# A kernel's own scheduler: small tiles tracked by the column, and fp32r matmuls counted as n + 32 cycles

## The chip, the cores and the metric

The kernel runs on one core of one Trainium2 chip. The metric is the device time of one execution in microseconds; the time before is 2639.61 us, the median of three runs (2639.43 to 2639.66).

## The reference, cut to what matters

Two transformer blocks follow each other on x of 256 tokens by 2048 channels, all in float32. The first has an input projection to 11,264 columns, a gated linear recurrence (HGRN2) and a banded attention with 8 heads each, two projections, an output projection and a feed-forward part of width 5632. The second takes a condition c, multiplies silu(c) by a 2048 x 12288 matrix, and uses the six pieces as shift, scale and gate:

```python
mod = jax.nn.silu(c) @ w_ada[l] + b_ada[l]
shift_m, scale_m, gate_m, shift_f, scale_f, gate_f = jnp.split(mod, 6, axis=-1)
h = modulate(rms_norm_2(x, pre_norm_mix[l]), shift_m, scale_m)
...                      # h @ w_in, two attention mixers with 8 heads each -> o_n, o_m
o = jnp.concatenate([o_n, o_m], axis=-1) @ w_o[l]
x = x + gate_m[:, None, :] * rms_norm_2(o, post_norm_mix[l])
h = modulate(rms_norm_2(x, pre_norm_ffn[l]), shift_f, scale_f)
f = jnp.square(jax.nn.relu(h @ w_up[l])) @ w_down[l]
x = x + gate_f[:, None, :] * rms_norm_2(f, post_norm_ffn[l])
```

Here w_o is 2048 x 2048, w_up 2048 x 8192 and w_down 8192 x 2048. A norm divides each token's row by the root of its mean square, so it needs the whole row of a product before the next product can begin.

## The kernel before, in words

**Products.** The 256 tokens are two blocks of 128 (tb 0 and 1). Every large product runs in groups of 512 output columns; a group's items are its 128-row chunks of the weight matrix. Activations and weights are each held as two fp32r halves, so an item is three matmuls per token block (`emit`: high by high, high by low, low by high) into an accumulator `acc` in PSUM. Weights come as pairs of chunks, 512 KB by one DMA into one of six `raw` buffers; ScalarE rounds them (`wh`) and VectorE subtracts (`wl`) into a ring of five to seven slots (`split_ahead`). How far ahead a pair is split is set by the count of items (`LA_AT`: 0, 2 or 4 items), not by a clock. Block 1 trails block 0 by `lag` items (14 at the end of w_o, 8 at the start of w_up, 4 elsewhere), at most lag + 6. A group that needs activations of a norm (`need`) waits for them. SP issues all DMAs.

**The planner.** The order on each engine is the order in which this Python program issues instructions, and semaphores keep it right whatever the order. The program issues with a model of the chip: a clock for each engine (`clk`: pe, at, dv, sp, dma), and for each piece of a tile when it was last written and read and by which engine (`wr`, `rd`). `op` starts an instruction when its engine is free and its operands are ready; a result of another engine counts 0.06 us later (`LAT`) beside a tail of 0.1 us (ScalarE, TensorE) or 0.05 us (VectorE). The pieces are 128 columns (`spans`). The costs are formulas: a 512-column VectorE operation is 512/960 + 0.068 = 0.601 us and 0.062 more with a per-row factor; a 512-column ScalarE operation from SBUF 512/1200 + 0.094, and 0.093 more for an accumulated sum; a DMA 1.1 us, then its bytes at 360 GB/s, then 1.5 us.

**Tasks.** Work beside the products is written as generators: each `yield` ends a step. A step is issued when TensorE's planned clock has reached its due time (`due`): after a plain yield, the planned end of what the step before it issued, plus 0.2 us; after `yield "dv"`, VectorE's planned clock less 0.2. `main` tries the splits first, then the tasks (`pump`), then the next item. Negative priorities go first.

**The norms between products.** After w_o (`post7`, `ev7`, `sums7`, lines from the function that opens phase 7): for each block, each 512 columns are squared on ScalarE with the sum into a column of `stat`, and multiplied by the gate on VectorE (og<-acc). Then `row_rstd` works out the factor in `stat`; four updates xr<-og,stat,xr on VectorE alternate with four squares og<-xr on ScalarE, whose sums go to other columns of `stat`; a second `row_rstd` follows; then `norm_mod` spawns four parts, each a scaling (og<-xr,stat, line 241), four transposes on TensorE (line 281), scale and shift, and the split into `hh` and `hl` that w_up's matmuls read. For block 0 the chain is issued in one go, for block 1 with a yield between its steps. `stat` is one tile of 128 x 64.

**gemv.** The product with w_ada runs on VectorE in 192 items of 512 KB (`gemv`, `gload`, tile graw): an item is started no sooner than 4.5 us of TensorE's planned clock after the one before it on a fixed schedule, and is issued when that clock has reached the planned landing of its load. It begins when the recurrence is done.

**Lines that the prediction touches.** Line 276 is the matmul in `mm`, 281 the transpose in `tr`, 220 every activation, 232, 236 and 241 VectorE's two-operand, scalar-and-tensor and scalar operations, 1438 the sum of four in `sum4`, 298 every DMA.

Of the kernel before, what the change touches and what calls it, by code (L numbers as in the profile page):

```python
# [85 lines left out]
class Group:  # L86
    def __init__(self, w, quads, c0, n, lhs, evac, need=None, lag=2, pre=None, name=""):
        self.w, self.quads, self.c0, self.n = w, list(quads), c0, n
        self.lhs, self.evac, self.need, self.lag, self.pre = lhs, evac, need, lag, pre
        self.chunks = [4 * q + j for q in self.quads for j in range(4)]  # L90
        self.acc = {}
        self.name = name
# [7 lines left out]
class Prog:  # L100
# [8 lines left out]
    def __init__(self, tc, ins, out, dbg=None, stop=99):  # L109
        self.tc, self.nc, self.ins, self.out, self.dbg, self.stop = tc, tc.nc, ins, out, dbg or {}, stop  # L110
        self.clk = {"pe": 0.0, "at": 0.0, "dv": 0.0, "sp": 0.0, "dma": 0.0}
        self.now = 0.0
        self.wr, self.rd, self.turn, self.place, self.bank = {}, {}, {}, {}, {}
        self.cur = 0.0
        self.set = None
        self.tasks = []
        self.queue = []
        self.done = set()
        self.hooks = []
        self.limits = {}  # L120
        self.items = []
        self.pairs = []
        self.p = [0, 0]
# [15 lines left out]
    def spans(self, ap):  # L139
        name = ap.tensor.name  # L140
        lo = hi = ap.offset
        for st, n in list(ap.ap)[1:]:
            if st < 0:
                lo += st * (n - 1)
            else:
                hi += st * (n - 1)
        p = self.place.get(name, name)
        return [(p, i) for i in range(lo // 128, hi // 128 + 1)]

    def ready_at(self, aps, eng):  # L150
        t = 0.0
# [117 lines left out]
    def mm(self, out, lhsT, rhs, start=True, stop=True):  # L269
        n = self.width(out)  # L270
        if lhsT.dtype == F32R:
            c = max(n + 6, 257 if n > 128 else 511)
        else:
            c = max(4 * n + 12, 1022 if n < 96 and self.width(lhsT) > 64 else 500)
        self.op("pe", c / 2400.0, [out], [lhsT, rhs])
        self.nc.tensor.matmul(out, lhsT, rhs, start=start, stop=stop)  # L276
# [306 lines left out]
    def tile(self, pool, shape, tag, bufs=1, dtype=F32):  # L583
        self.uid += 1
        t = pool.tile(list(shape), dtype, tag=tag, name=f"{tag}_{self.uid}", bufs=bufs)
        self.slot(t, pool, tag, bufs)
        return t

    def pool(self, name, side):
# [1337 lines left out]
```

## Time and profile before

| | |
|---|---|
| median of three runs | 2639.61 us |
| the profiled execution | 2640.57 us |
| its span, first to last instruction | 2638.8 us |
| mean granted TensorE clock | 0.997 |
| matmul and transpose records on TensorE | 12084 |

The profile is of one execution. A busy TensorE is not one at its peak, since the ends of its matmuls are modelled; the distance between starts tells more. A wait is put down to the engine that came last.

### The profile page before, as it was taken

Reading aid. Unit: us, or ns where it says so; the run is one execution under the profiler, and the core shown is the slowest. Engines: PE = TensorE matmul, PEld = TensorE weight load, DVE = VectorE, ACT = ScalarE, POOL = GpSimd, SP = SyncE. Lnnn points to the kernel's source line nnn. Section 1 sums busy time; section 2 is a strip of 40 time slices with the busy share of each in tenths; the row PEclk is TensorE's granted clock in tenths of the full one; section 3 lists DMA queues with packets and bytes.
Section 4 is the critical chain, followed back from the end, with each engine's and each line's share of the span. In section 5 each row is a group of like instructions: output and inputs, shape, how many; then the busy total and the mean of one; then the engine's idle time right before and its main releaser. Section 6 shows DMA issues by size and latency. Waiting matters only on the chain.

```text
span 2638.8 us, 32635 instructions
## 1 busy us (share of the span) xinstructions
PE 2608.0 (99%) x12084; PEld 2155.7 (82%) x12084; DVE 1733.8 (66%) x2408; ACT 1241.3 (47%) x1756; POOL 0.2 (0%) x4
## 2 busy tenths in 40 slices
PE   8999999999999999999999999999999999999998
PEld 7888888888888888888888887888778888888887
DVE  6665668888778888888854655655554444444445
ACT  7565555444453434333443543554554454453443
POOL 0000000000000000000000000000000000000000
PEclk9999999999999999999999999999999999999999
DMA  7545448888779889998955465345355555556553
GB/s 275 184 143 164 163 155 288 308 296 292 262 243 318 311 296 326 333 333 307 317 194 190 138 225 169 127 136 191 135 185 185 197 182 193 189 180 197 184 183 130
DMA packets 163888, 582.00 MB, mean 221 GB/s; under 512 B 18448, under 2 KB 19984, under 8 KB 163472
## 3 DMA queue, kind: packets, MB, share of 16 engines
q1 hardware_dynamic: 163728, 579.91, 64.4%
q8 instruction: 95, 1.56, 0.2%
q14 instruction: 65, 0.53, 0.1%
HBM read 577.74 MB, written 2.10 MB: 220 GB/s over the span
## 4 chain that ended last, share of the span: by engine, by line
PE 89%; DVE 4%; DMA 4%; ACT 2%; issue 1%; SPq 0%; DVEq 0%; ACTq 0%
PE acc L276 83%; PE s L276 4%; DMA graw<-in_w_ada 3%; PE s L281 2%; DVE wl L232 1%; DVE gacc L236 1%; ACT wh L220 0%; PE d L276 0%; PE d L281 0%; DMA ident<-in_cst 0%; DVE A L267 0%; DMA raw<-in_masks 0%; DMA raw<-in_w_in 0%; ACT evt L220 0%; DVE evt L232 0%
## 5 line engine op out<-in xcount | busy, mean ns | idle before, releaser
L232 DVE TENSOR_TENSOR wl<-raw,wh 128x1024 fp32r<-128x1024 f32 (+2 forms) x875 | 1043.4, 1210 | 543.8 <-ACT wh L220 541.7
L220 ACT ACTIVATE wh<-raw 128x1024 fp32r<-128x1024 f32 (+2 forms) x875 | 897.1, 1047 | 610.4 <-PE acc L276 565.8
L276 PE MATMUL acc<-wh,hh 128*128 128x512 f32 (+2 forms) x1600 | 629.6, 393 | 4.0 <-ACT hh L220 3.4
L276 PE MATMUL acc<-wh,hl 128*128 128x512 f32 (+2 forms) x1600 | 618.2, 386 | 0.9 <-DVE hl L232 0.9
L276 PE MATMUL acc<-wl,hh 128*128 128x512 f32 (+2 forms) x1600 | 617.3, 386 | 1.5 <-DVE wl L232 1.5
L276 PEld LDWEIGHTS acc<-wh,hh 128*128 128x128 f32 x1600 | 301.0, 188 | 67.2 <-issue 5.2
L276 PEld LDWEIGHTS acc<-wh,hl 128*128 128x128 f32 x1600 | 300.7, 188 | 63.4 <-DVE hl L232 2.1
L276 PEld LDWEIGHTS acc<-wl,hh 128*128 128x128 f32 x1600 | 301.3, 188 | 59.0 <-DVE wl L232 2.2
L236 DVE SCALAR_TENSOR_TENSOR gacc<-graw,csilu,gacc 128x512 f32<-128x512 f32 x360 | 269.9, 750 | 45.8 <-DMA graw<-in_w_ada 38.2
L276 PE MATMUL acc<-wh,xh 128*128 128x512 f32 x704 | 282.4, 401 | 6.5 <-ACT wh L220 6.5
L276 PE MATMUL acc<-wl,xh 128*128 128x512 f32 x704 | 275.6, 392 | 0.9 <-DVE wl L232 0.9
L276 PE MATMUL acc<-wh,xl 128*128 128x512 f32 x704 | 275.8, 392 | 0.0
L276 PE MATMUL acc<-wh,uh 128*128 128x512 f32 x512 | 200.0, 391 | 0.0
L276 PE MATMUL acc<-wh,ul 128*128 128x512 f32 x512 | 199.3, 389 | 0.0
L276 PE MATMUL acc<-wl,uh 128*128 128x512 f32 x512 | 199.2, 389 | 0.0
L276 PEld LDWEIGHTS acc<-wh,xh 128*128 128x128 f32 x704 | 133.0, 189 | 32.1 <-ACT wh L220 6.5
L276 PEld LDWEIGHTS acc<-wl,xh 128*128 128x128 f32 x704 | 133.0, 189 | 27.9 <-DVE wl L232 2.1
L276 PEld LDWEIGHTS acc<-wh,xl 128*128 128x128 f32 x704 | 132.7, 188 | 28.2
L276 PE MATMUL acc<-wh,fh 128*128 128x512 f32 x320 | 125.0, 391 | 0.0
L276 PE MATMUL acc<-wh,fl 128*128 128x512 f32 x320 | 124.6, 389 | 0.0
L276 PE MATMUL acc<-wl,fh 128*128 128x512 f32 x320 | 124.5, 389 | 0.0
L276 PEld LDWEIGHTS acc<-wh,ul 128*128 128x128 f32 x512 | 96.1, 188 | 20.0
(283 smaller groups left out, 2426.7 us busy)
## 6 DMA issues: line engine op xcount, KB each, us to landing
raw<-in_w_in SPq DMA_DIRECT2D x255, 512.0 KB, 4.0
graw<-in_w_ada SPq DMA_DIRECT2D x192, 512.0 KB, 5.1
raw<-in_w_ffn_in SPq DMA_DIRECT2D x176, 512.0 KB, 5.0
raw<-in_w_up SPq DMA_DIRECT2D x128, 512.0 KB, 4.2
raw<-in_w_down SPq DMA_DIRECT2D x128, 512.0 KB, 4.2
raw<-in_w_ffn_out SPq DMA_DIRECT2D x88, 512.0 KB, 4.9
raw<-in_w_out SPq DMA_DIRECT2D x32, 512.0 KB, 4.4
raw<-in_w_o SPq DMA_DIRECT2D x32, 512.0 KB, 4.3
```

Of the source, the lines that this page charges most:

```text
L220: self.nc.scalar.activation(out=out, in_=in_, func=func, **kw)
L232: self.nc.vector.tensor_tensor(out=out, in0=a, in1=b, op=op)
L236: self.nc.vector.scalar_tensor_tensor(out=out, in0=a, scalar=s, in1=b, op0=op0, op1=op1)
L276: self.nc.tensor.matmul(out, lhsT, rhs, start=start, stop=stop)
L281: self.nc.tensor.transpose(out, in_, self.ident[:p, :p])
```

## The change

`spans` gives the pieces of a tile by which the planner keeps reads and writes apart. Two-dimensional tiles of at most 64 columns are now kept column by column; wider ones by 128 columns as before. `mm` counts an fp32r matmul of n columns as n + 32 cycles of 2.4 GHz where it counted n + 6. Both are bookkeeping: the instructions are the same, and only the order in which they are issued can differ.

```diff
--- before.py
+++ after.py
@@ -110,6 +110,7 @@
         self.tc, self.nc, self.ins, self.out, self.dbg, self.stop = tc, tc.nc, ins, out, dbg or {}, stop
         self.clk = {"pe": 0.0, "at": 0.0, "dv": 0.0, "sp": 0.0, "dma": 0.0}
         self.now = 0.0
+        self.small = set()
         self.wr, self.rd, self.turn, self.place, self.bank = {}, {}, {}, {}, {}
         self.cur = 0.0
         self.set = None
@@ -145,7 +146,8 @@
             else:
                 hi += st * (n - 1)
         p = self.place.get(name, name)
-        return [(p, i) for i in range(lo // 128, hi // 128 + 1)]
+        u = 1 if name in self.small else 128
+        return [(p, i) for i in range(lo // u, hi // u + 1)]
 
     def ready_at(self, aps, eng):
         t = 0.0
@@ -269,7 +271,7 @@
     def mm(self, out, lhsT, rhs, start=True, stop=True):
         n = self.width(out)
         if lhsT.dtype == F32R:
-            c = max(n + 6, 257 if n > 128 else 511)
+            c = max(n + 32, 257 if n > 128 else 511)
         else:
             c = max(4 * n + 12, 1022 if n < 96 and self.width(lhsT) > 64 else 500)
         self.op("pe", c / 2400.0, [out], [lhsT, rhs])
@@ -584,6 +586,8 @@
         self.uid += 1
         t = pool.tile(list(shape), dtype, tag=tag, name=f"{tag}_{self.uid}", bufs=bufs)
         self.slot(t, pool, tag, bufs)
+        if len(shape) == 2 and shape[1] <= 64:
+            self.small.add(t.tensor.name if hasattr(t, "tensor") else t.name)
         return t
 
     def pool(self, name, side):
```

## Rows read from the trace of the kernel before

**Rows 1.** The page of the whole execution: the busy time of each engine (us, share of the span, number of instructions).

```profile
PE 2608.0 (99%) x12084; PEld 2155.7 (82%) x12084; DVE 1733.8 (66%) x2408; ACT 1241.3 (47%) x1756; POOL 0.2 (0%) x4
```

**Rows 2.** The chain of work that ended last, in order of time, over the whole span: start us, length us, what ran, how many in a row. One of its long unbroken pieces, in the w_up and w_down products.

```profile
2191.13 102.73 PE acc L276 x453
```

**Rows 3.** What TensorE waited for in the whole run: engine, tile and line, what it waited for, us in total, how often, the longest in us. Four of them, the largest among them.

```profile
PE acc L276 <- ACT wh L220: 7.1, 2, 6.5
...
PE acc L276 <- DVE wl L232: 2.4, 4, 0.8
PE s L281 <- DVE og L241: 2.2, 1, 2.2
PE s L281 <- DVE stat L1438: 2.0, 1, 2.0
```

**Rows 4.** Busy time by stage: the stretch in us from the span's start, its length, then the busy time and number of instructions of each engine, the granted TensorE clock, the DMA engines' busy share and GB/s.

```profile
950.00:1190.00 240.00, 238.93 (x1063) 197.28 (x1062) 212.81 (x259) 95.23 (x96) 0.00 (x0) 1.00 0.91 324
1480.00:1500.00 20.00, 18.02 (x82) 14.46 (x81) 16.65 (x26) 13.81 (x28) 0.00 (x0) 0.93 0.30 93
1895.00:1930.00 35.00, 25.70 (x107) 18.76 (x106) 26.92 (x44) 22.34 (x47) 0.00 (x0) 0.90 0.31 106
2010.00:2280.00 270.00, 270.00 (x1210) 223.49 (x1209) 127.02 (x116) 120.55 (x134) 0.00 (x0) 1.00 0.58 192
```

**Rows 5.** ScalarE in order of time around 2114 us, inside a w_up product: start us, length us, engine, line, operation, out<-in, shapes, count, and in brackets the idle time before it and what ended it.

```profile
2114.55 0.63 ACT L220 ACTIVATE ut<-ut 128x512 f32<-128x512 f32 x1
```

**Rows 6.** TensorE in order of time around 2114 us (columns as in rows 5).

```profile
2115.53 0.39 PE L276 MATMUL acc<-wh,hl 128*128 128x512 f32 x1
2115.76 0.60 PE L281 MATMUL s<-ident,ut 128*128 128x128 f32 x4
```

**Rows 7.** VectorE in order of time around the end of the w_o product (columns as in rows 5).

```profile
1889.91 2.74 DVE L236 SCALAR_TENSOR_TENSOR xr<-og,stat,xr 128x512 f32<-128x512 f32 x4
...
1894.29 0.41 DVE L236 SCALAR_TENSOR_TENSOR stat<-stat 128x1 f32<-128x1 f32 x2 [0.51 <-ACT stat L220]
1895.24 1.23 DVE L232 TENSOR_TENSOR wl<-raw,wh 128x1024 fp32r<-128x1024 f32 x1 [0.54 <-ACT wh L220]
1898.15 0.69 DVE L232 TENSOR_TENSOR og<-acc,gg 128x512 f32<-128x512 f32 x1 [1.68 <-ACT gt L220]
1898.76 0.48 DVE L241 TENSOR_SCALAR og<-xr,stat 128x512 f32<-128x512 f32 x1
...
1902.69 0.75 DVE L236 SCALAR_TENSOR_TENSOR xr<-og,stat,xr 128x512 f32<-128x512 f32 x1
...
1909.53 5.76 DVE L232 TENSOR_TENSOR wl<-raw,wh 128x1024 fp32r<-128x1024 f32 x5
1915.20 2.07 DVE L236 SCALAR_TENSOR_TENSOR xr<-og,stat,xr 128x512 f32<-128x512 f32 x3
```

**Rows 8.** ScalarE in order of time, the same stretch (columns as in rows 5): the square of block 1's last w_o result.

```profile
1897.43 0.60 ACT L220 ACTIVATE gt<-acc 128x512 f32<-128x512 f32 x1 [2.22 <-PE acc L276]
```

**Rows 9.** TensorE in order of time from 1896 to 1905 us (columns as in rows 5).

```profile
1897.00 0.39 PE L276 MATMUL acc<-wh,ol 128*128 128x512 f32 x1
1899.38 3.64 PE L281 MATMUL s<-ident,og 128*128 128x128 f32 x16 [1.99 <-DVE stat L1438]
1904.09 0.50 PE L276 MATMUL acc<-wh,hh 128*128 128x512 f32 x1 [1.07 <-ACT hh L220]
```

**Rows 10.** The chain in order of time at the earlier border, 1470 to 1506 us (columns as in rows 2): twelve transposes.

```profile
1476.46 1.39 PE s L281 x12
```

**Rows 11.** TensorE in order of time from 1903 to 1926 us (columns as in rows 5).

```profile
1905.42 0.50 PE L276 MATMUL acc<-wh,hl 128*128 128x512 f32 x1 [0.60 <-DVE hl L232]
...
1907.20 0.49 PE L276 MATMUL acc<-wh,hh 128*128 128x512 f32 x1 [0.58 <-ACT wh L220]
1908.46 0.50 PE L276 MATMUL acc<-wl,hh 128*128 128x512 f32 x1 [0.77 <-DVE wl L232]
...
1910.80 0.50 PE L276 MATMUL acc<-wl,hh 128*128 128x512 f32 x1 [0.69 <-DVE wl L232]
...
1917.28 0.39 PE L276 MATMUL acc<-wh,hl 128*128 128x512 f32 x1
1919.91 3.47 PE L281 MATMUL s<-ident,og 128*128 128x128 f32 x16 [2.24 <-DVE og L241]
1924.48 0.50 PE L276 MATMUL acc<-wh,hh 128*128 128x512 f32 x1 [1.11 <-ACT hh L220]
...
1925.49 0.50 PE L276 MATMUL acc<-wh,hl 128*128 128x512 f32 x1 [0.27 <-DVE hl L232]
```

**Rows 12.** The tile graw (the rows of w_ada on their way through VectorE), 950 to 1190 us: engine, operation, count, duration in ns (least, median, most), first and last start in us; and the time from a load's issue to its landing.

```profile
L236 DVE SCALAR_TENSOR_TENSOR gacc<-graw,csilu,gacc x116: 741/752/754, 950.0 to 1188.9; 128x512 f32<-128x512 f32 x116
L298 SPq DMA_DIRECT2D graw<-in_w_ada x62: 327/328/1347, 951.6 to 1189.7; - x62
...
DMA to landing us min/median/max: 3.2/5.1/7.2
```

**Rows 13.** What VectorE waited for between 950 and 1190 us (columns as in rows 3): the largest.

```profile
DVE gacc L236 <- DMA graw<-in_w_ada: 17.8, 17, 2.1
```

**Rows 14.** The page's costliest groups: line, engine, operation, out<-in, count, busy us, mean ns of one, idle before it and what ended it. The two halves of a weight split.

```profile
L232 DVE TENSOR_TENSOR wl<-raw,wh 128x1024 fp32r<-128x1024 f32 (+2 forms) x875 | 1043.4, 1210 | 543.8 <-ACT wh L220 541.7
L220 ACT ACTIVATE wh<-raw 128x1024 fp32r<-128x1024 f32 (+2 forms) x875 | 897.1, 1047 | 610.4 <-PE acc L276 565.8
```

## The prediction

> **What bounds the kernel now.** I read the page's busy lines first, then the chain of work in order of time, then TensorE's waits, then busy time by stage. The page shows a TensorE that is busy 99% of the span [rows 1]; since ends of matmuls are modelled, that alone proves little. The chain gives the rate: 453 matmuls of 512 columns that wait for nothing take 102.73 us [rows 2], 226.8 ns each, which is 544 cycles at 2.4 GHz, 512 + 32. The 10,656 fp32r matmuls (counted from the code's groups; 192 of them are about half as wide) make some 2,400 us at that rate, 91% of the span, and the change alters none of them. TensorE's waits name what is left: the largest single ones are 6.5 us at the start, and about 2 us each where the norm after the w_o product stands between two matrix products [rows 3]. By stage, the two such borders show up as the only late stretches with a real gap: 18.0 of 20 us busy at 1480 to 1500, 25.7 of 35 us at 1895 to 1930, both with a granted clock under 1, against 270.0 of 270 us in the long w_up/w_down stretch [rows 4]. So the time is TensorE's own work plus a few gaps; a planner's bookkeeping can only move the gaps.
>
> **Part 1: n + 32 in place of n + 6.** The planner counted 518 cycles (0.2158 us) for a matmul that takes 544 (0.2267 us), so its TensorE ran 5.0% ahead of the chip's. After the change it agrees with [rows 2] to within a cycle. No instruction is added or removed. What moves is where a task's next step is put into TensorE's order: a step due x planner us later is now x/0.2267 matmuls later, not x/0.2158.
> The Trainium skill speaks against this edit: "TensorE: Matmul & The Clock Gate", Back-to-back issue gap, lists 518 cycles for a free size of 512, just the old n + 6. By that figure, as an estimate, the same 453 matmuls would take 97.8 us; the trace has 102.73, so for these fp32r matmuls the old count was wrong and the new one right.
> In a stretch where TensorE never waits, steps that come sooner gain nothing. They can lose: the input must be ready. In w_up, the square that a transpose reads ends at 2115.18 [rows 5] and the transpose starts at 2115.76 [rows 6], 0.58 us of slack, of which one matmul, 0.23 us, may go. That is safe here. Where slack is thinner a wait appears. I bound it: the code has some 230 such steps (62 splits of activations, 32 heads with four to eleven steps each, the norms). If one in eight, 30, has under 0.25 us of slack and loses up to 0.2 us, that is 6 us; so 0 to +6. The one-in-eight is my choice. The waits that TensorE has now on small steps are 1 us a kind or less, so I take a value near the lower end, **+0.5 us**.
>
> **Part 2: small tiles by the column.** `stat` (128 x 64) holds every norm's sums and factors, and was one key, so the planner made any reader of one column wait for the last writer of any other. The effect is plainest after w_o, in `post7`. There, four pairs of an x update on VectorE (xr) and a square on ScalarE alternate. The square adds its sum to a column of stat; the next xr reads another column. The planner saw a wait: 0.663 + 0.11 + 0.614 + 0.16 = 1.55 us a pair (VectorE's cost, tail and latency, ScalarE's, tail and latency). The chip sees none: the four xr run back to back in 2.74 us [rows 7].
> Worked out from the planner's costs, for token block 0, counted from its last w_o matmul: sums and first rstd 2.3 us; four pairs, the last square's sum visible at 8.4; second rstd ready at 9.3. Block 1's last matmul comes 42 matmuls later (LAG7 = 14 items of three), 42 x 0.2158 = 9.06. So the planner held the factor to be ready only when TensorE was done; it put the wl of the next pair in between, and then block 1's own evacuation, ahead of the scaling that feeds the transposes. The trace shows what that order costs: the factor is there at 1894.70, wl ends at 1896.47, VectorE then sits until block 1's evacuation at 1898.15, and the scaling (og<-xr) starts only at 1898.76 [rows 7], because the evacuation waits for ScalarE's square of the last matmul's result [rows 8]. TensorE's last w_o matmul starts at 1897.00, it transposes from 1899.38, and has its first w_up matmul at 1904.09 [rows 9].
> After: the squares follow each other, 0.614 us apiece, the second rstd is ready at 6.5, wl ends at 8.4, and the scaling comes due at 8.2, while TensorE's end is now at 42 x 0.2267 = 9.52. So the scaling is put about six matmuls ahead of the end, in front of the evacuation. On the chip it can then start when wl ends, 1896.5 instead of 1898.76: 2.3 us. The 16 transposes, 3.64 us now [rows 9] at the lower of the two clock levels for most of their run, run nearer to the full one (12 took 1.39 us at the earlier border [rows 10], so 16 would take 1.85), and part of the 1.8 us lies on the path: I take 0.7 us. TensorE will wait about 1.3 us for the scaling with six matmuls of block 1 still to do; those fill the gap afterwards, so this wait only changes places. Sum of the first gap: **-3.0 us**. Bounds: 0, if block 1's delayed evacuation gives it all back in the second gap, to -9.3, the idle time of both gaps, 1.99 + 1.07 + 0.60 + 0.58 + 0.77 + 0.69 in the first and 2.24 + 1.11 + 0.27 in the second [rows 9, 11].
> The second gap I leave as it is. There TensorE ends block 0's 14 items at 1917.28 and restarts at 1924.48 [rows 11]; block 1's chain made its first xr at 1902.69 but its other three only at 1915.20, behind five wl [rows 7]. That order comes from splits being issued greedily ahead of tasks, which the change does not touch.
>
> **Part 3: what else moves.** The gemv of w_ada is paced by the planner's TensorE clock, and, where it is behind that schedule, by the planned landing of its loads, so it gets 5.0% denser: some 3 more of its 62 items between 950 and 1190 [rows 12]. The splits (1.05 us on ScalarE, 1.21 on VectorE [rows 14]) are issued by item count, not by the clock, so they do not move. VectorE has 27 us free there [rows 4], TensorE is the cover: 0 us, price under the rivals. At the border of 1480 to 1500 no square alternates with an update through stat; 0 +- 1 us.
>
> **Sum:** -3.0 + 0.5 = -2.5 us. The profiled execution took 2640.57 us, 1.8 more than its span and 0.04% over the runs' median of 2639.61; I subtract from the median: **2637.1 us**. A measurement here tells 0.2% (5.3 us) from nothing, so this counts as no change.
>
> **Rivals.**
> A, both gaps close: if block 1's xr chain is put ahead of the splits as well, the 12.7 us of waits and slow transposes between 1897 and 1926 (9.3 us of idle, 3.4 us of 3.64 + 3.47 over 2 x 1.85 [rows 9, 11]) shrink by two thirds: -8.5, 2631 us. For it: every step of that chain reads stat, and with false waits gone each step is due sooner. Against it: the starving of 1903 to 1915 is by splits. Chance 0.28, all of it faster.
> B, slower: VectorE becomes the bound under the gemv. Between 950 and 1190 it is busy 212.8 of 240 us [rows 4] and waits 17.8 us for graw [rows 13]. Three more items cost 3.1 x 2 x 0.75 = 4.7 us. A load's planned 4.06 us (1.1 + 1.46 + 1.5 in the code) now spans 4.26 real us and then 4.06, while the median landing is 5.1 [rows 12], so up to 65 waits get 0.2 us longer, 13 us. 212.8 + 17.8 + 4.7 + 13 = 248 us in 240: TensorE would wait 8 us for wl, 2648 us. It decides from the point where this sum passes 240. Against it: a VectorE that is late finds its load landed, so the 13 and the 17.8 shrink as fast as it falls behind, and TensorE waits only 2.4 us for wl in the whole run [rows 3]. Chance 0.08.
> C, thin slack: with TensorE counted right and ScalarE and VectorE still counted short (0.947 and 1.135 in the code against 1.05 and 1.21 [rows 14]), the old error had cancelled part of theirs. All 30 thin steps wait: +6, less the 3 gained, 2642 to 2646. Chance 0.08, half of it slower. If the skill's 518 cycles held, this would reach every step; the chain's rate leaves that no chance of its own.
> That the new sets change nothing (a name that doesn't match) is out: the name stored is the one that `spans` looks up. Forecast: chance 0.56, own range 2634.5 to 2641.
>
> **Numbers.** Faster 0.28 (A), same 0.60 (forecast 0.56, half of C), slower 0.12 (B, half of C). The range 2630 to 2643 takes in A's centre and C's nearer half and leaves about a tenth on either side.
>
> **What would show it.** Right: transposes of og among w_o's last matmuls; first w_up matmul some 3 us sooner against w_o's end; VectorE's og<-xr ahead of og<-acc; graw's last issue some 40 us sooner; the same 226.8 ns a matmul. Wrong: new waits of TensorE on wl while the gemv runs (B), a long list of 0.1 to 0.3 us waits on small steps (C), or a block 1 chain with its four xr together (A). A different order in the attention stages that gains or loses over 5 us would be something I have not priced.

## The result, and the profile after

The changed kernel takes **2672.84 us** (median of four runs, 2668.83 to 2676.13) against 2639.64 for the kernel before beside it: a ratio of 1.0124 (95% interval 1.0111 to 1.0137), 33 us slower. The forecast was 2637.1, and its range ended at 2643. The profiled execution took 2676.13 us, its span 2674.0, so the two traces differ by 35.2 us.

The page's busy lines come first, to be read against [rows 1]:

```profile
PE 2624.3 (98%) x12084; PEld 2156.4 (81%) x12084; DVE 1734.8 (65%) x2408; ACT 1240.8 (46%) x1756; POOL 0.2 (0%) x4
```

The number of instructions is the same on every engine, and so is the busy time of VectorE and ScalarE to a microsecond. Nothing was added; TensorE waits more, and part of its work runs at the lower clock after waits (mean granted clock 0.994, where it was 0.997). The chain's unbroken piece in the w_up and w_down products is the same too (start us, length us, what ran, how many), where [rows 2] had 102.73:

```profile
2226.42 102.72 PE acc L278 x453
```

What TensorE waited for in the whole run (tile and line, what it waited for, us in total, how often, the longest in us), against [rows 3]:

```profile
PE s L283 <- DVE fs L238: 8.3, 8, 2.0
PE acc L278 <- ACT wh L222: 7.7, 2, 6.2
PE acc L278 <- DVE wl L234: 5.9, 11, 0.8
PE s L278 <- DVE gpart L1553: 5.0, 3, 3.9
PE s L283 <- DVE g L234: 4.1, 5, 1.4
PE s L283 <- DVE og L243: 3.9, 2, 3.6
```

The wait for ScalarE is the old one at the start of the run. The others that are new or longer name VectorE. Two of them are not the gemv's: og is at the border of w_o, and of the 5.9 us for wl only 2.0 lie between 391 and 1320 us, where the gemv runs. In that stretch before had two such waits, 1.6 us in all:

```profile
PE s L276 <- DVE gpart L1549: 1.1, 2, 0.8
PE s L281 <- DVE g L232: 0.5, 1, 0.5
```

After has all of fs, gpart and g there, and these four for wl, 19.4 us together:

```profile
PE acc L278 <- DVE wl L234: 2.0, 4, 0.8
```

Waits that name one engine through many tiles suggest that the engine is late, rather than that one step is badly placed.

To find the place, I took each stage by its own first and last matmul, since the two traces drift apart and a fixed window holds different work. From TensorE's start times, in us:

| stage | before | after | n + 32 alone | columns alone | no gemv, before | no gemv, after |
|---|---|---|---|---|---|---|
| w_in, first part | 379.9 | 382.3 | 380.5 | 380.3 | 378.8 | 381.0 |
| w_in, second part, and heads | 272.3 | 280.4 | 277.9 | 271.7 | 273.0 | 276.1 |
| w_out | 91.0 | 91.0 | 92.0 | 91.1 | 91.0 | 91.0 |
| ffn of the first layer, part 0 | 399.3 | 415.9 | 412.8 | 399.3 | 398.0 | 398.0 |
| ffn of the first layer, part 1 | 334.7 | 339.5 | 337.9 | 335.0 | 333.1 | 333.2 |
| w_in of the second layer | 319.8 | 322.4 | 320.7 | 319.4 | 319.8 | 321.1 |
| w_o | 100.7 | 96.5 | 100.1 | 98.1 | 100.7 | 96.5 |
| w_up and w_down, to the end | 734.7 | 739.9 | 734.7 | 737.2 | 734.7 | 739.0 |

29.5 us of the 35 (8.1 + 0 + 16.6 + 4.8) lie in the stages in which the gemv of w_ada runs (390 to 1310 us in before); 3.2 of them (3.1 + 0 + 0 + 0.1) come without the gemv as well, by the last two columns. The border at w_o, on which the forecast spent its work, gained 4.2 us and gave 5.2 back.

The worst stage, in busy time by stage (columns as in rows 4). First of before, the stretch in which 1,728 matmuls and their transposes run, then of after, the same work:

```profile
750.00:1149.00 399.00, 398.73 (x1787) 329.79 (x1786) 349.81 (x428) 167.79 (x180) 0.00 (x0) 1.00 0.89 315
```

```profile
760.00:1176.00 416.00, 405.18 (x1790) 331.44 (x1790) 369.08 (x459) 167.89 (x181) 0.00 (x0) 0.99 0.90 317
950.00:1190.00 240.00, 233.99 (x1023) 191.68 (x1022) 214.53 (x262) 92.38 (x93) 0.00 (x0) 0.99 0.92 325
```

For the same matrix work VectorE has 31 instructions more (459 against 428) and 19.3 us more busy time; TensorE, which had stopped for 0.3 us in all, now loses 17 us: 10.8 in which it is not busy, and the rest mostly at the lower clock behind the stops. VectorE's waits for graw in these two stretches are, before and after:

```profile
DVE gacc L236 <- DMA graw<-in_w_ada: 20.9, 25, 2.1
```

```profile
DVE gacc L238 <- DMA graw<-in_w_ada: 30.2, 34, 2.9
```

Busy and waiting together were 349.8 + 20.9 = 370.7 us of 399; now they are 369.1 + 30.2 = 399.3, just TensorE's own need of 399. Rival B's sum is there, but not made as B had it: most of the rise is work (19.3 us), less of it waits (9.3 us). The tile graw between 950 and 1190 us, against [rows 12]: 123 multiply-adds for 116, 66 loads for 62.

```profile
L238 DVE SCALAR_TENSOR_TENSOR gacc<-graw,csilu,gacc x123: 741/752/755, 950.0 to 1188.4; 128x512 f32<-128x512 f32 x123
L300 SPq DMA_DIRECT2D graw<-in_w_ada x66: 327/328/441, 950.8 to 1189.2; - x66
...
DMA to landing us min/median/max: 3.5/5.0/6.5
```

One loss as it happens, in order of time, all engines, 1261 to 1268 us of after (columns as in rows 5):

```profile
1261.96 0.39 PE L278 MATMUL acc<-wh,hl 128*128 128x512 f32 x1
1262.35 0.48 DVE L243 TENSOR_SCALAR gacc<-graw,csilu 128x512 f32<-128x512 f32 x1
...
1262.87 0.75 DVE L238 SCALAR_TENSOR_TENSOR gacc<-graw,csilu,gacc 128x512 f32<-128x512 f32 x1
1263.54 0.74 DVE L238 SCALAR_TENSOR_TENSOR fs<-acc,stat,fg 128x512 f32<-128x512 f32 x1
1263.64 0.33 SPq L300 DMA_DIRECT2D graw<-in_w_ada  x1
...
1264.33 0.66 PE L283 MATMUL s<-ident,fs 128*128 128x128 f32 x4 [1.98 <-DVE fs L238]
...
1265.52 0.59 PE L278 MATMUL acc<-wh,hh 128*128 128x512 f32 x1
...
1265.92 0.63 PE L278 MATMUL acc<-wl,hh 128*128 128x512 f32 x1
...
1266.08 1.54 DVE L238 SCALAR_TENSOR_TENSOR gacc<-graw,csilu,gacc 128x512 f32<-128x512 f32 x2 [0.67 <-DMA graw<-in_w_ada]
1266.34 0.63 PE L278 MATMUL acc<-wh,hl 128*128 128x512 f32 x1
```

VectorE runs its list in order: two gemv steps stand ahead of fs, TensorE waits 1.98 us for fs, and from 1265.92 to 1268.90 its matmuls start 0.42 to 0.43 us apart instead of 0.227, at the lower clock level. The clock is the number before the last two (columns as in rows 4):

```profile
1266.00:1268.00 2.00, 2.00 (x6) 1.57 (x5) 1.89 (x3) 1.51 (x2) 0.00 (x0) 0.50 0.97 367
```

The load that follows is issued at 1263.64, right behind the multiply-add that ended at 1263.62 and so gave its buffer back. At 1266.08 VectorE has already waited 0.67 us for graw.

### The profile page after: what moved, and what is told of

Read it like the earlier page. It is cut to its first block, busy times and chain, and to the rows that moved or that the text cites. A ratio compares the mean times of both kernels' runs of the same rounds, so it can differ in the third digit from the quotient of the medians.

```text
span 2674.0 us, 32646 instructions
## 1 busy us (share of the span) xinstructions
PE 2624.3 (98%) x12084; PEld 2156.4 (81%) x12084; DVE 1734.8 (65%) x2408; ACT 1240.8 (46%) x1756; POOL 0.2 (0%) x4
## 4 chain that ended last, share of the span: by engine, by line
PE 75%; DVE 11%; DMA 9%; issue 3%; ACT 2%; SPq 0%; DVEq 0%; ACTq 0%
PE acc L278 69%; DMA graw<-in_w_ada 7%; DVE wl L234 4%; PE s L278 4%; DVE gacc L238 3%; PE s L283 2%; ACT wh L222 1%; DVE graw L1551 0%; ACT og L222 0%; DMA raw<-in_w_in 0%; DMA raw<-in_w_ffn_in 0%; DVE gpart L1553 0%; PE d L278 0%; PE d L283 0%; DVE g L234 0%
```

## The experiments

Twelve kernels, in three groups. Ratios are to the kernel before on the same chip, with 95% intervals. The theory was that the gemv's schedule is the place and VectorE the engine; the rivals were steps with too little slack all over the run, the border at w_o, traffic of the loads, and the density of the multiply-adds by itself.

**1. Which edit, and with or without the gemv.**

`only_n32`, the cycle count alone:

```
-            c = max(n + 6, 257 if n > 128 else 511)
+            c = max(n + 32, 257 if n > 128 else 511)
```

> Only the count of n + 32; small tiles stay one key. Theory 1 (TensorE counted at its true rate takes away the 5% by which VectorE's short costs and graw's late landings had been covered, so VectorE falls behind while the gemv runs): 2660 to 2675 us, with 20 to 30 us more of TensorE waiting between 400 and 1320 us. Rival (the finer keys reorder the stretch): 2640 us, within 4 us of the kernel before.

Measured: 2664.78 us, ratio 1.0090 (1.0075 to 1.0105), so +24 us.

`only_small`, the columns alone:

```
+        self.small = set()
...
+        u = 1 if name in self.small else 128
+        return [(p, i) for i in range(lo // u, hi // u + 1)]
...
+        if len(shape) == 2 and shape[1] <= 64:
+            self.small.add(t.tensor.name if hasattr(t, "tensor") else t.name)
```

> Only the keys by the column; n + 6 stays. Theory 1: 2634 to 2641 us, the same as before or the 3 us that the prediction gave to the norm after w_o. Rival (the finer keys are what costs): 2660 to 2673 us.

Measured: 2641.08 us, ratio 1.0003 (0.9994 to 1.0012): nothing. The count makes most of the loss. Together the edits lose 33, some 8 more than the count alone. By the table (whose traces differ by 11) they are spread over the run: 1.8 + 2.5 us in the first w_in, 3.1 + 1.6 in the ffn, 1.7 in the second w_in, 1.6 at the border of w_o, 1.0 less in w_out. Why the columns cost this beside the new count and nothing beside the old one is not shown.

`nogemv_before` and `nogemv_after`, the gemv's work taken out of either kernel (in after, the same lines):

```
-                    while self.pe < start + n * self.gemv_pace or not self.gload(n, pool):
-                        yield "wait"
...
+                    if j == 0:
+                        t = self.tile(pool, [128, 2, 512], "graw", 2)
+                        self.fill(acc, 0.0)
```

> The kernel before with the gemv's 192 loads of w_ada and its 384 multiply-adds left out (a fill takes their place, so the six pieces are the bias alone). Theory 1: TensorE hardly waited there before, so 2632 to 2640 us.

> The changed kernel with the same left out. Theory 1: the loss sits in the gemv's stretch, so this comes to within 5 us of the kernel before without its gemv. Rival (steps with thin slack wait everywhere, gemv or not): 15 us or more over it.

Measured: 2637.27 us, ratio 0.9987 (0.9977 to 0.9996), and 2645.6 us, ratio 1.0017 (1.0008 to 1.0027). The change costs 8.3 us without the gemv and 33 with it, so about 25 come through the gemv. The 8.3 are over the 5 that I allowed: the two traces differ by 6.4 us, and by the table above 6.6 us lie in the three w_in stages (2.2 + 3.1 + 1.3), while the w_o border gives 4.2 and takes 4.3. In part 0 of the ffn nothing is left, 398.0 us in both.

**2. What in the gemv.**

`no_load_after`, the changed kernel with the loads of w_ada left out and every multiply-add kept in its place (both of an item read the same half of one of two tiles that are filled once):

```
-            t = self.tile(pool, [128, 2, 512], "graw", 2)
-            self.dma(t, self.block("w_ada", 256 * j, c0, 512))
+            t = self.gheld[n % 2]
+            self.dma(t, self.block("w_ada", 256 * j, c0, 512), real=False)
...
+                            self.stt(acc, t[:, 1], c, acc, OP.mult, OP.add)
```

> The changed kernel with all of the gemv's VectorE work, its schedule and its planned landings kept, but the 192 loads of w_ada left out: the multiply-adds read two tiles that are filled once. Theory 2a (VectorE falls behind because it sits waiting for graw's late landings, which the planner does not count): VectorE's waits for graw are gone, and the time is 2644 to 2651 us, near the 2645.6 of the changed kernel without the gemv. Theory 2b (VectorE's own work got too dense): 2658 to 2672 us, with TensorE still waiting some 15 us or more for VectorE between 400 and 1320 us.

Measured: 2645.29 us, ratio 1.0021 (1.0010 to 1.0031), the level of the changed kernel without any gemv (2645.6). Its stretch with the same 1,728 matmuls, by stage and by tile:

```profile
752.00:1151.00 399.00, 398.90 (x1788) 329.89 (x1787) 364.82 (x458) 168.01 (x180) 0.00 (x0) 1.00 0.56 190
```

```profile
L238 DVE SCALAR_TENSOR_TENSOR gacc<-graw,csilu,gacc x197: 742/750/754, 768.8 to 1150.9; 128x512 f32<-128x512 f32 x197
```

and the tile's line of after in its own 416 us:

```profile
L238 DVE SCALAR_TENSOR_TENSOR gacc<-graw,csilu,gacc x198: 741/752/755, 776.8 to 1175.7; 128x512 f32<-128x512 f32 x198
```

VectorE has as much to do in 399 us as after had in 416, and TensorE loses nothing. So the density alone does no harm; it needs the loads as well, by the waits for them or by their traffic, which is taken up below.

`land_late`, a load's data counted as landed 1.5 us later, which moves the multiply-adds back behind other work:

```
-                    while self.pe < self.gt[n]:
+                    while self.pe < self.gt[n] + 1.5:
```

> The changed kernel; only, the planner lets an item of the gemv wait 1.5 us more than its planned landing. Theory 2a: VectorE's waits for graw between 950 and 1190 us fall from 18.6 to under 8 us, and the time to 2644 to 2656 us. Theory 2b: better as well if the items thin out by as much (then the count of items between 950 and 1190 us falls well under 62); with 62 or more items it would stay over 2660.

Measured: 2646.49 us, ratio 1.0025 (1.0015 to 1.0036): nearly all of the gemv's loss is gone. But not only in the way I meant. Between 950 and 1190 us VectorE still waits for graw, 15.5 + 1.2 us where I had expected under 8, and the loads went down to 61 from 66, so this edit also made the gemv thinner (96 loads in the ffn's part 0, where after has 106 and before 95). It can't part the two theories:

```profile
DVE gacc L238 <- DMA graw<-in_w_ada: 15.5, 15, 2.4
DVE gacc L243 <- DMA graw<-in_w_ada: 1.2, 1, 1.2
```

```profile
L300 SPq DMA_DIRECT2D graw<-in_w_ada x61: 327/328/994, 956.7 to 1189.2; - x61
```

`gemv_as_before` and `gemv_as_after` were to stretch the two delays that pace the gemv by 544/518 in after, and to shrink them by 518/544 in before:

```
-        self.gemv_pace = 4.5
+        self.gemv_pace = 4.5 * K
...
-            self.gt[n] = self.wr[self.spans(t)[0]][0]
+            self.gt[n] = self.pe + K * (self.wr[self.spans(t)[0]][0] - self.pe)
```

> The changed kernel with the gemv's two delays on TensorE's planned clock (4.5 us between items, and the time from issue to planned landing) stretched by 544/518, so that they span as many real us as before the change. If the loss comes through the gemv's own clock: 2645 to 2655 us. If it comes from the other steps being due sooner while VectorE is as late as it always was: 2662 to 2672 us.

> The kernel before (n + 6, one key for a small tile) with the same two delays shortened by 518/544, so that the gemv alone gets as dense in real time as after the change. If the loss comes through the gemv's own clock: 2652 to 2665 us. If it needs the other steps to be due sooner: 2639 to 2645 us.

Measured: 2670.66 us, ratio 1.0108 (1.0082 to 1.0134), and 2641.03 us, ratio 0.9997 (0.9987 to 1.0007). Neither took the other's time. Neither took the other's density either: in the ffn stage's part 0 the first has 103 loads where after has 106 and before 95, the second 98. The runs say that these two delays don't set the density; on the density itself they are inconclusive. Both times lie in the ranges of the second theory, the other steps due sooner (2662 to 2672 and 2639 to 2645 us); as the densities did not change places, that is no proof of it, but it isn't excluded either. One reason why the pace of 4.5 us had no say there: both kernels have finished 56 items when part 0 begins (112 multiply-adds in either trace, by 749.7 and by 759.8 us), some 20 items or more behind the schedule of the gemv (an estimate, from the time since its first load over 4.5 planned us), so all through part 0 the gemv is catching up.

**3. How much room the loads need, and a better version.**

`half_after`, four buffers of 256 KB, three loads ahead, in place of two of 512 KB, one ahead (the same memory):

```
-            t = self.tile(pool, [128, 2, 512], "graw", 2)
+            t = self.tile(pool, [128, 512], "graw", 4)
...
-                    self.gload(n + 1, pool)
+                        for a in range(1, 4):
+                            self.gload(n + a, pool)
```

> The changed kernel with the gemv's two buffers of 512 KB cut into four of 256 KB and a load for each, three ahead: the same bytes and the same multiply-adds in the same room, but a buffer comes free after one multiply-add, and three loads are under way while VectorE works on the fourth. Theory 2a (a load starts only when VectorE gives its buffer back, so a late VectorE makes its own next load late): VectorE's waits for graw between 950 and 1190 us fall to under 8 us from 18.6, and the time to 2645 to 2655 us. Rival 2c (more than the wait for graw: steps come too soon for VectorE's order in any case): over 2662 us.

Measured: 2656.99 us, ratio 1.0062 (1.0047 to 1.0077): half of the loss is gone, between the two ends that I gave. The theory's own sign failed: VectorE's waits between 950 and 1190 us are 19.3 us, not under 8 (18.6 in after). So a buffer that is given back late is not all that makes VectorE wait, and why this edit gives half of the loss back is not shown.

`land_half`, as land_late with 0.75 us:

> The changed kernel with 0.75 us instead of 1.5 us added to the planned landing. If VectorE's own sum (busy and waiting for graw, per unit of TensorE's work) has to fall below TensorE's time, the loss goes in one step near that point, and the time lies at either end, 2646 to 2652 or 2664 to 2672 us; if each wait costs its own share, half way: 2655 to 2663 us.

Measured: 2652.69 us, ratio 1.0047 (1.0031 to 1.0064). Half the delay gives back three quarters of what the whole one did (20 of 26 us, by the medians), so the loss isn't in proportion to the delay; the time lies 0.7 us over the lower of the two ends. But part 0 has 96 loads here as in land_late, so the edit is not half way in density, and that the loss goes in one step is not shown.

`small_la0`, the columns with the old count, and no splits ahead at the borders that stand second in the table of lookaheads:

```
-LA_AT = {-2: 0, -1: 2, 0: 4}
+LA_AT = {-2: 0, -1: 0, 0: 4}
```

> The kernel before (n + 6) with the keys by the column, and no split ahead of need while the second token block's norm is under way (LA_AT for priority -1 from 2 to 0), so that its four updates are not held up behind splits after w_o. If the second gap after w_o is those splits' doing: 3 to 5 us off TensorE's stretch from the last w_o matmul on, 2634 to 2638 us. If TensorE then waits for its own splits instead: 2639 to 2645 us.

Measured: 2637.74 us, ratio 0.9994 (0.9984 to 1.0003): not to be told from before, though the profiled execution spends 2.1 us less from the w_o stage on (98.1 + 735.2 us against 100.7 + 734.7).

`half_small_la0`, that with the four half buffers:

> Both at once on n + 6: keys by the column, four half buffers for the gemv, no split ahead of need in the second block's norm. What TensorE still waited for VectorE in the gemv's stretch of the kernel before is some 3 us, so 2631 to 2637 us if both work; 2638 to 2645 us if neither moves it.

Measured: **2634.86 us**, ratio 0.9977 (0.9968 to 0.9987), as expected: 5 us faster than the kernel before and 38 faster than the changed one. At the w_o border block 1's xr are one by one between splits, where [rows 7] had three of them behind five wl (VectorE), and the transposes wait 0.35 us where [rows 11] had 2.24 (TensorE):

```profile
1905.22 0.75 DVE L238 SCALAR_TENSOR_TENSOR xr<-og,stat,xr 128x512 f32<-128x512 f32 x1
...
1907.03 0.74 DVE L238 SCALAR_TENSOR_TENSOR xr<-og,stat,xr 128x512 f32<-128x512 f32 x1
...
1908.86 0.74 DVE L238 SCALAR_TENSOR_TENSOR xr<-og,stat,xr 128x512 f32<-128x512 f32 x1
...
1910.66 0.74 DVE L238 SCALAR_TENSOR_TENSOR xr<-og,stat,xr 128x512 f32<-128x512 f32 x1
```

```profile
1914.41 1.50 PE L283 MATMUL s<-ident,og 128*128 128x128 f32 x12 [0.35 <-DVE og L243]
```

**All of them in one stage.** Part 0 of the ffn, the same 1,728 matmuls and their transposes, which take TensorE 399 us when nothing is late. VectorE's busy time and its waits for graw in that stretch of each trace, in us (from the stage's own first to its last matmul and with all waits for graw, so the sums of before and after are 2.1 and 0.5 us above those of the fixed windows):

| kernel | stage | VectorE busy | waits for graw | sum |
|---|---|---|---|---|
| no_load_after | 399.3 | 365.5 | 0 | 365.5 |
| land_late | 398.9 | 350.8 | 18.2 | 369.0 |
| before | 399.3 | 351.0 | 21.8 | 372.8 |
| only_small | 399.3 | 348.7 | 25.7 | 374.4 |
| small_la0 | 398.9 | 348.0 | 26.5 | 374.5 |
| half_small_la0 | 398.8 | 359.5 | 16.7 | 376.1 |
| land_half | 402.1 | 353.1 | 24.4 | 377.5 |
| gemv_as_after | 399.4 | 354.2 | 26.0 | 380.2 |
| half_after | 410.2 | 360.7 | 28.2 | 388.9 |
| gemv_as_before | 410.6 | 362.0 | 36.6 | 398.6 |
| after | 415.9 | 369.6 | 30.2 | 399.8 |
| only_n32 | 412.8 | 364.0 | 35.9 | 399.9 |

The rows are sorted by the sum, and the stage's time follows it in the main: up to 380 the loss is nothing, or 3 us in one row, and from 389 on it is 11 to 17. VectorE's busy time alone doesn't sort them: no_load_after (365.5) and half_small_la0 (359.5) lose nothing, gemv_as_before (362.0) and half_after (360.7) lose 11. The waits alone do as well as the sum (up to 26.5 without a loss, from 28.2 on with one, and the same row of 3 us out of line), so the table can't tell whether the sum or the waits are the measure; the sum says why waits hurt here, where the room is small. It is VectorE's need for the work set against TensorE's, not a utilisation: in the slow rows the stage is longer than the 399 us. One pair says more than the order. half_after and half_small_la0 have the same 208 half loads in this stage and nearly the same busy time (360.7 and 359.5 us), but 28.2 and 16.7 us of waits, and 11 us of loss and none. They differ in the count and in the lookahead, and the lookahead by itself changed nothing here (small_la0 against only_small). So at one density the new count still adds waits: how soon the steps come is a part of the cause, and the runs don't part the gemv's own steps from the others.

Weight loads held up behind those of w_ada, since SP issues both in one list, are out: in the windows of before and after shown above, ScalarE waits for no raw load. Traffic of the loads as a cause by itself is out: half_small_la0 moved more per second than after, at a higher DMA share, with TensorE busy throughout:

```profile
750.00:1149.00 399.00, 399.00 (x1789) 330.35 (x1788) 359.19 (x449) 168.05 (x180) 0.00 (x0) 1.00 0.93 326
```

## Why the prediction was wrong

**The failed step is the dismissal of rival B.** The mechanism stood there, with its sum (248 of 240 us) and its point; I gave it 0.08 because "a VectorE that is late finds its load landed, so the 13 and the 17.8 shrink as fast as it falls behind". That takes the load's issue as fixed in time. It isn't. With two buffers, a load is issued when VectorE gives one back: of the loads of the items 60 to 191, 87 to 88% in both traces are issued within 0.2 us of that, with a median of 28 ns (worked out from each load's start and the end of the multiply-add before it on that buffer). So a late VectorE makes its own next load late by as much, and the landing, 5.0 us [after's graw] as against 5.1 [rows 12], comes on top again. The waits went up with the lateness, 20.9 to 30.2 us, instead of down; for one load that is 0.22 us and then 0.28 (95 and 106 loads). That the loads matter is shown by no_load_after, where they and with them the waits are gone, the multiply-adds stay, and the loss goes. How much of the waits this chain of buffer and load makes is not shown: half_after loosened it, and its waits stayed.

B's sum was right by luck in its parts: it put 4.7 us of work and 13 of waits on top in 240 us, and part 0 has 19.3 and 9.3 in 399, which is 11.6 and 5.6 in 240. Its price, 2648 us, was for one stretch of 240 us; the gemv runs for some 900.

**The mis-sized term is part 3, "TensorE is the cover: 0 us"; it measured about 25.** The room was read right (27 us free in [rows 4]), but set against the extra 4.7 us alone; the 17.8 us of waits [rows 13] were taken for free time, when they were time in which VectorE, in order, could do nothing else. Room less waits was 9 us in 240. And the density was under-estimated: the forecast had 5% by the count; the loads in the same work show 11.6% (106 against 95). The gemv was behind its schedule there, so its pace, on which the 5% rested in the first place, did not space the items. The traces don't show why the density rose by more than the count did, and the two experiments meant for it did not reach it. It stays open.

**Part 1, +0.5 us (0 to +6).** Without the gemv the three w_in stages lose 6.6 us by the two edits together, and only_small loses nothing in them with it (380.3 + 271.7 + 319.4 against 379.9 + 272.3 + 319.8). Thin slack fits this, just over the upper bound and not near the lower one, but is shown for about half of it: TensorE's waits that are new there are of 0.2 to 0.7 us each and come to 0.4 + 2.0 + 1.3 = 3.7 us; the rest shows in no wait. That only_small is so clean makes the count, or the count together with the columns, the cause; the runs don't part the two without the gemv.

**Part 2, the first gap, -3.0 us.** The mechanism came as forecast. TensorE around the end of w_o, 1930 to 1935 us of after, against [rows 9]:

```profile
1930.54 0.39 PE L278 MATMUL acc<-wh,ol 128*128 128x512 f32 x1
1931.23 1.50 PE L283 MATMUL s<-ident,og 128*128 128x128 f32 x12 [0.30 <-DVE og L243]
1932.48 0.47 PE L278 MATMUL acc<-wh,oh 128*128 128x512 f32 x1
...
1933.26 0.60 PE L283 MATMUL s<-ident,og 128*128 128x128 f32 x4
1934.11 0.50 PE L278 MATMUL acc<-wh,hh 128*128 128x512 f32 x1 [0.26 <-ACT hh L222]
```

Transposes stand among w_o's last matmuls, their wait is 0.30 us instead of 1.99, and the stage takes 4.2 us less. **The second gap, "I leave as it is", didn't stay.** VectorE and then TensorE of after at that place, against [rows 7, 11]:

```profile
1946.61 2.36 DVE L234 TENSOR_TENSOR wl<-raw,wh 128x1024 fp32r<-128x1024 f32 x2
1948.88 2.74 DVE L238 SCALAR_TENSOR_TENSOR xr<-og,stat,xr 128x512 f32<-128x512 f32 x4
...
1953.71 1.68 DVE L243 TENSOR_SCALAR og<-xr,stat 128x512 f32<-128x512 f32 x4
```

```profile
1954.25 3.37 PE L283 MATMUL s<-ident,og 128*128 128x128 f32 x16 [3.55 <-DVE og L243]
```

The four xr stand together, the sign that I had named for rival A, but behind six wl (two of them shown) instead of ahead of the splits: the wait grew from 2.24 to 3.55 us. The next stage took 5.2 us more, so the border gave +1.0 in all, over the bound of 0, "if block 1's delayed evacuation gives it all back in the second gap". The longer wait is 1.3 of the 5.2. Another 3 us are w_up's first matmuls, which now run partly at the lower clock where the transposes did before (by stage, before and then after, columns as in rows 4):

```profile
1904.00:1920.00 16.00, 11.05 (x43) 7.67 (x44) 13.35 (x21) 10.34 (x20) 0.00 (x0) 1.00 0.58 196
```

```profile
1934.00:1954.00 20.00, 14.22 (x42) 9.22 (x42) 15.54 (x26) 12.91 (x28) 0.00 (x0) 0.83 0.49 159
```

So what the transposes gained nearer to the full clock, 0.7 us in the forecast, the matmuls behind them gave back.

**Rival C's reason was wrong as well.** Two wl back to back take 2.36 us and five 5.76 [rows 7], so one starts 1.14 us after the other, near the planner's 1.135, although one alone shows 1.21. ScalarE's six wh there start 0.95 us apart, as the planner's 0.947 has it, at 1.05 each:

```profile
1906.09 5.79 ACT L220 ACTIVATE wh<-raw 128x1024 fp32r<-128x1024 f32 x6
```

The planner's costs were not short; I compared a rate with a duration. For VectorE, the Trainium skill, "Vector Engine (DVE) Microarchitecture Reference", 5.2 Measured stream behaviour, gives 1.0417 ns a column and about 75 ns an instruction for such a row of instructions; as an estimate that is 1.14 us for 1024 columns, and the trace agrees with its 1.14.

Of the signs I had named, graw's last issue came 27.7 us sooner (1282.9 against 1310.6), not 40; the stages themselves got longer. And new waits of TensorE on wl while the gemv ran, the sign for B, are there with 2.0 us; the longer ones on fs, gpart and g I had not named.

## What to carry to other kernels

When an engine runs its list in order and its loads are issued as it frees the buffers, don't take its waits for them as free time: add them to its busy time, and compare the sum with what the bounding engine needs. That the sum, and not the waits alone, is the measure is not shown; here no loss up to a sum of 0.95 of that need (380 of 399 us), with one row of 3 us just below, and 11 us at 0.97. A cost that is corrected in a planner moves everything that is paced by the planned clock, the background work too, so look first at how much room the engine under that work has. Before a rival is dismissed because lateness heals itself, look at what issues the next load: a clock, or the late engine.

## What was not expected of the hardware

- Back to back, VectorE's instructions start closer than they last: wl of 128x1024 every 1.14 us at 1.21 each [rows 7, 14], four xr of 128x512 in 2.74 us [rows 7] at 0.75 each (1905.22 above).
- At the lower clock level an fp32r matmul of 512 columns follows the one before after 0.42 to 0.43 us (1265.92, 1266.34 above, granted clock 0.50), 512 cycles at 1.2 GHz within the rounding, while at the full one it takes 544 [rows 2]: the 32 cycles on top show at the full clock only.
